# Two products opened together behind constant matmuls, and lo parts and last sums in another order

## The chip, the cores and the metric

The kernel runs on one core of a Trainium2 chip. The metric is the device time of one execution in microseconds (us), the median of several runs; less is better.

## The reference

Two layers of a streaming encoder work on 640 tokens (512 of a new stream, 8 × 16 of running ones) of width D = 1024. Each layer has a half feed-forward, a mixer and another half feed-forward. All is float32. Cut to what this change touches:

```python
def _rmsnorm(x, g):
    xf = x.astype(jnp.float32)
    y = xf * lax.rsqrt(jnp.mean(xf * xf, axis=-1, keepdims=True) + EPS)
    return y.astype(x.dtype) * g
def _swiglu(h, w_gu, w_down):
    gu = h @ w_gu
    g, u = jnp.split(gu, 2, axis=-1)
    return (jax.nn.silu(g) * u) @ w_down
...
    for l in range(DEPTH):            # DEPTH = 2, D_FF = 2816
        xp = xp + 0.5 * _swiglu(_rmsnorm(xp, norm_ffn1[l]), w_ffn1_gu[l], w_ffn1_down[l])
...
        xp = xp + mp                  # mixer: short convolution and banded attention
        xp = xp + 0.5 * _swiglu(_rmsnorm(xp, norm_ffn2[l]), w_ffn2_gu[l], w_ffn2_down[l])
```

## The kernel before, in words

**Layout and accuracy.** x lies transposed: eight blocks of 128 rows of D by 640 tokens. Each float32 operand of a matmul is split in a hi part, which ACT (ScalarE) casts, and a lo part, the rest, which DVE (VectorE) subtracts. A product of one 128 × 128 block is three products on PE (TensorE): hi·hi, lo·hi and hi·lo, each as two matmuls of 320 tokens. Names: `whi`, `wlo` are a slab's parts, `xhi`, `xlo` a block's. A trailing a or b in a name stands for the feed-forward ahead of or behind the mixer.

**Slabs.** Weights come from `wst` as slabs of 128 × 1024 that SP's queue loads into three `raw` buffers. Line 368 casts a slab's hi part on ACT at once. Its lo part is put in a list, which `flush` (line 374) hands to DVE when the program calls it. A slab in the set `fine` has its lo part cut in two halves there. Some slabs are sums or differences of others; DVE makes them (line 297), or a DMA that accumulates does, issued by POOL (`lent`, lines 276 and 277).

**Products by seven.** Past the opening, gate and up products of the feed-forward and the down products are made in a scheme with seven block products in place of eight. The kinds are X11, X21, XT5, XN6, XT7, X22 and XT4; X sums and differences of operands are made for it (`mixed`, `even`, `odd`, `rest`, `fourth`), and partial results in PSUM go to `c` tiles and into others.

**Down products.** `down_rows` adds a chunk's product to four rows of D. It runs X11, X21, XN6, XT5, XT7, X22, XT4 through the accumulators `da`, `db` and `dc`. A result goes to x in one of two ways: `take` (line 1196) is two DVE operations that add it straight from PSUM; `send` (line 1191) has ACT scale it into a tile and POOL issue two DMAs that add it to x. Two takes of `da` (columns t2, then t1), one of `dc`, and the sends of c1, c5, u2 belong to each group. The first half of `da` must be out before XT4 may write it: the matmul `daa<-t4hia` waits there. There are ten groups in each feed-forward, named by first chunk and first row (0_0, 0_4, 4_0, … 16_4).

**The opening** (line 752) is the first feed-forward's first eight products, plain ones, made while x arrives: product 0 over the eight x blocks, then 1, and so on, 48 matmuls each, through two accumulators, `po`. So product 2 waits until ACT has copied product 0 out (`out(0)`, line 786), product 3 for product 1's copy (line 794). A product takes the raw x; the norm's factor comes in later, on the results. Its sums of squares (ACT line 731, DVE line 297) are totalled over partitions by 20 small matmuls (`npsa`, line 552) within product 2, turned by DVE and spread by two matmuls (`nbca`, line 571) within product 3.

**Order.** PE's order is the program's. ACT's and DVE's are as written too for most of the program; for a part of it a scheduler sets them. SP's queue holds the loads in order, and POOL's holds the accumulating DMAs.

Of the kernel before, what the change touches and what calls it, by code (L numbers as in the profile page):

```python
# [16 lines left out]
P = 128  # L17
# [177 lines left out]
def trunk(ctx: ExitStack, tc: tile.TileContext, xin, wst, small, pbias, samplebias, kcache, vcache, gfin,  # L195
# [27 lines left out]
    def att(name):  # L223
        return banks["att"].tile([P, 512], F32, tag="att", name=name)
# [33 lines left out]
    raws, ready = [], []  # L258
    rows = [what == "rows" for l in range(L) for k in "ab" for what, _ in ffn_order(f"{k}{l}") if what in ("gu", "rows")]
    fine = {i + o for i, r, before in zip([i for i, z in enumerate(slabs) if z[0] == "gu" and z[2] == 0], rows,  # L260
                                          [False] + rows) if r for o in ((1, 3) if before else (3,))}
    sums, pool, spool = {}, [None], [None]
    lent, lean, at = {}, set(), 0
    for name, (_, units) in zip([f"{k}{l}" for l in range(L) for k in "amb"], stages()):
# [107 lines left out]
    def flush(n=None):  # L372
        for lo, src, hi in pending[:n]:
            DVE.tensor_tensor(out=lo, in0=src, in1=hi.bitcast(F32), op=ALU.subtract)  # L374
        del pending[:n]
# [20 lines left out]
    def ahead():  # L396

        source(len(ready))
# [92 lines left out]
    for k in range(KT):  # L491
        SP.dma_start(x[k], xin[:, k, :])

        if k == 0:
            raws.append(wp.tile([P, CH], F32, tag="raw", name="raw0", bufs=3))
        if k % 2 == 0:
            c = slice(k * P, (k + 2) * P)
            SP.dma_start(raws[0][:, c], wst[0][:, c])

    def norm(name, goff, ssum, keep):  # L500

# [82 lines left out]
    class Expand(Stats):  # L584
# [98 lines left out]
        def mixed(self, kp):  # L683

            n = f"{self.name}_{kp}"
            hi, lo = self.ops[kp]
            (e1, e2), (o1, o2) = ([x[2 * kp + i][:, c] for c in (slice(0, HT), slice(HT, T))] for i in range(2))
            ge, go = (sm[:, self.goff + 2 * kp + i :][:, 0:1] for i in range(2))
            no = less1[:, 2 * kp + 1 : 2 * kp + 2]
            E = self.fp.tile([P, 3, HT], F32, name=f"xe{n}", tag="even", bufs=1)  # L690

            def minus(out, a, g, b):
                DVE.scalar_tensor_tensor(out=out, in0=a, scalar=g, in1=b, op0=ALU.mult, op1=ALU.subtract)

            ACT.activation(E[:, 2], e2, AF.Copy, scale=ge)
            minus(E[:, 1], e1, ge, E[:, 2])
            self.flush()
            ACT.copy(hi[:, XT5], E[:, 1])
            self.late.append((lo[:, XT5], E[:, 1], hi[:, XT5]))
            yield  # L700
            self.flush()
            O = self.fp.tile([P, 5, HT], F32, name=f"xo{n}", tag="odd", bufs=1)
            minus(O[:, XN6], o2, no, E[:, 1])
            minus(O[:, XT4], o1, no, O[:, XN6])
            minus(O[:, XT7], o2, go, E[:, 2])
            ACT.copy(hi[:, 0:3], O[:, 0:3])
            self.late.append((lo[:, 0:3], O[:, 0:3], hi[:, 0:3]))
            yield
# [46 lines left out]
    def opening(fp, name, goff, n, pairs, tails):  # L755

        ACT.copy(early, epst)
        ex = Expand(fp, name, goff)  # L760
        h = []
        whi, wlo = (wp.tile([P, CH], F32R, tag=f"w{t}", name=f"w{t}0", bufs=3) for t in ("hi", "lo"))
        ready.append((whi, wlo))
        for k in range(KT):
            h.append(ex.plain(k))
            c = slice(k * P, (k + 2) * P)
            if k % 2 == 0:
                ACT.copy(whi[:, c], raws[0][:, c])
                DVE.tensor_tensor(out=wlo[:, c], in0=raws[0][:, c], in1=whi[:, c].bitcast(F32),
                                  op=ALU.subtract)  # L770
        flush()

        mixed = [z for kp in range(NP) for z in [ex.mixed(kp)] * 2]
        made = {2: (0, 1, 2), 3: (3,), 4: (4,), 5: (5, 6), 6: (7,)}
        us, gs, ps = [], [], []

        def out(i):

            j, up = divmod(i, 2)
            if not up:  # L780
                gs.append(tmp(f"g{name}_{j}"))
                if j:
                    scaled(gs[j], ps[i], ex.rho)
                    ACT.activation(gs[j], gs[j], AF.Silu)
                else:
                    ACT.copy(halves(gs[j]), two(ps[i]))
                return
            u = tmp(f"u{name}_{j}") if j > 1 else fp.tile([P, T], F32, tag="cap", name=f"u{name}_{j}", bufs=6)
            us.append(u)
            if j:  # L790
                scaled(u, ps[i], ex.rho)
                DVE.tensor_tensor(out=u, in0=u, in1=gs[j], op=ALU.mult)
            else:
                ACT.copy(halves(u), two(ps[i]))

        def begun():
            ex.total(att(f"nps{name}"))
            ex.root()
            ex.diagonal()

        at = {2: {4: begun}, 3: {1: lambda: ex.spread([att(f"nbc{name}_{a}")[:, :HT] for a in range(2)])}}
        for i in range(2 * n):
            ps.append(acc(f"po{name}_{i}"))
            product(ps[i], h, at.get(i, {}))
            if i > 1:
                out(i - 1)
            if i == 0:
                for k in range(KT):
                    ex.square(k)
                    ex.add()  # L810
                    if k == 1:
                        out(0)
                    if k == 4:
                        flush()
            if i == 1:
                continue
            if i == 3:
                g, u = gs[0], us[0]
                DVE.tensor_tensor(out=g, in0=g, in1=ex.rho, op=ALU.mult)
                ACT.activation(g, g, AF.Silu)  # L820
                DVE.tensor_tensor(out=u, in0=u, in1=ex.rho, op=ALU.mult)
            flush()
            for m in made.get(i, ()):
                next(mixed[m])
            if i == 3:
                DVE.tensor_tensor(out=u, in0=u, in1=g, op=ALU.mult)
            if i == 4:
                pairs[0].even(us[0])
            if i == 5:
                pairs[0].odd(us[1])  # L830
            if i == max(made):
                ex.flush()
                ahead()
                pairs[0].mixed()
                pairs[0].fourth()
            if i == 2 * n - 1:
                pairs[1].even(us[2])
        ahead()
        out(2 * n - 1)
        tails += [lambda: pairs[1].odd(us[3]), pairs[1].mixed, pairs[1].fourth]  # L840
        ex.rest = None
        return ex
# [46 lines left out]
    def gate_up(fp, n, ex, first, tails, put, j, pair, later, at, halve):  # L889
# [9 lines left out]
        def spot(name):  # L899
            step(later, f"g{at}{name}")  # L900
# [4 lines left out]
        both = cap("c1_")  # L905
        c1, u2, c5 = both[:, 0], both[:, 1], cap("c5_")[:, 0]
        rho = ex.rho
        early_down = False
        if first:

            new = not ex.known
# [34 lines left out]
                tails.clear()  # L946
            s2 = quiet()
            prep(len(ready))
            if new:
                flush()  # L950

            def third():
                mul(pc, s2, 1, X22, every, False, True)
# [2 lines left out]
            if new:  # L956
                third()
                ex.total(acc(f"nps{n}")[:, 0])
                ex.root()
                ex.diagonal()  # L960
                prep(len(ready))
            mul(pa, s2, 0, XT7, every, False, True)
            add(g[:, t2], pa, c5)
# [5 lines left out]
            if not new:  # L969
                third()  # L970
                prep(len(ready))
                flush()
                held.extend(tails)
                tails.clear()
            s3 = slab(True)[0]
        else:
# [13 lines left out]
            flush()  # L990
            mul(pa, s1, 0, XN6, every, False, True)
            ACT.copy(u2, pa)
            early_down = len(held) > 2
            for t in held[: 1 if early_down else None]:
                t()
            del held[: 1 if early_down else None]
# [6 lines left out]
            add(g[:, t2], pa, c5)  # L1003
            DVE.tensor_tensor(out=g[:, t2], in0=g[:, t2], in1=rho[:, t2], op=ALU.mult)
            flush()
            if early_down:
                held.pop(0)()
            ahead()
            mul(pc, s2, 1, X22, every, False, True)
            add(u[:, t2], pc, u2)  # L1010
# [5 lines left out]
        if early_down:  # L1016
            behind.append(silu)
        else:
            silu()
        spot("e7")  # L1020
        flush()

# [21 lines left out]
    class Pair:  # L1044
# [64 lines left out]
        def fourth(self):  # L1109

            hi, lo = (self.fp.tile([P, HT], F32R, tag=f"t4{i}{self.i}", name=f"t4{i}{self.name}", bufs=1)
                      for i in ("hi", "lo"))
            ACT.copy(hi, self.A[:, 1])
            self.low(lo, hi, self.A[:, 1])
            self.keep((XT4,), hi, lo)

        def low(self, lo, hi, z):
            DVE.tensor_tensor(out=lo, in0=z, in1=hi.bitcast(F32), op=ALU.subtract)
# [31 lines left out]
                next(p.work)  # L1150
                p.done += 1

    def down_rows(fp, n, ms, pairs, tails, later):


        A, B = (acc(f"d{i}{n}") for i in "ab")
# [36 lines left out]
        def take(ps, r, cols, scale=0.5):  # L1193
            for u in range(2):
                xs = x[ms[2 * u + r]][:, cols]
                DVE.scalar_tensor_tensor(out=xs, in0=ps[u], scalar=scale, in1=xs, op0=ALU.mult, op1=ALU.add)
# [36 lines left out]
        s3 = slab(True)[0]  # L1233
        ahead()
        mul(a, s3, 0, XT4, False)
        take(a, 1, t1, -0.5)
        flush()

    def ffn(name, fp, ex, goff, after, end=False):
# [54 lines left out]
        for what, a in ffn_order(name):  # L1294
# [20 lines left out]
                continue  # L1315
            if what == "rows":
                ms, js = a
                down_rows(fp, f"{name}_{js[0]}_{ms[0]}", ms, [pairs[j] for j in js[::2]], tails, later)
                continue
            js = a if what == "ends" else a[0][1]  # L1320
            if js[0] == last or len(a) * len(js) >= KT:
# [1148 lines left out]
```

## Time and profile before

| | before |
|---|---|
| median of 3 runs | 2471.61 us (2471.43 to 2471.65) |
| profiled execution | 2472.6 us |
| its span | 2470.8 us |
| instructions | 44076 |
| PE busy | 2458.0 us |
| DVE busy | 2195.4 us |
| ACT busy | 1399.7 us |
| POOL busy | 326.8 us |
| moved by DMA | 290.26 MB |

The profile shows one execution; its span runs from the first instruction to the last, and 1.8 us of the execution's time lie outside it. Times in a row are us from the start of the span. A row of a timeline gives start, duration, engine, line, operation, tiles, and in brackets the idle time ahead of it and what ended it; "x2" means two instructions put together. A matmul's duration is its whole passage and overlaps the next one's; the pace is read from starts. A row of the table by stretches gives for each engine the busy time and the number of instructions, then the granted clock of PE, the DMA share and GB/s. In a row of waits stand the engine and tile that waited, what it waited for, the total, the number and the longest.

### The profile page before, as it was taken

The page shows a single profiled execution, that of the slowest core. Times are in us where ns is not written, and L with a number is a line of the kernel's source. Part 1 is how long each engine was busy: PE and PEld are TensorE (multiplying, and loading weights), DVE is VectorE, ACT ScalarE, POOL GpSimd, SP SyncE. Part 2 cuts the span into 40 slices and gives each one's busy share as a digit, 9 for nine tenths or more (in the row PEclk, how much of TensorE's full clock was granted, in tenths as well). Part 3 has the DMA queues.
Part 4 walks back from the last instruction along what each step waited for, and adds up shares of the span by engine and source line. Part 5 has one row for each costly group of instructions (what it writes and reads, how often), then busy time and mean ns, then how long its engine had stood idle before and what let it go on. Part 6 is the DMA issues. An engine that isn't in the chain of part 4 may idle for free.

```text
span 2470.8 us, 44076 instructions
## 1 busy us (share of the span) xinstructions
PE 2458.0 (99%) x17216; PEld 2407.4 (97%) x17216; DVE 2195.4 (89%) x3726; ACT 1399.7 (57%) x2242; POOL 326.8 (13%) x491
## 2 busy tenths in 40 slices
PE   9999999999999999999999999999999999999999
PEld 8999999889999999999999999998899999999998
DVE  7999998888998899998799999998889989999997
ACT  6555556675565555555665555567656555555555
POOL 0110112211110001111001010121110000111111
PEclk9999999999999999999999999999999999999999
DMA  4443445335344334444334343452454433444444
GB/s 156 127 117 103 118 118 128 104 120 175 108 131 125 90 102 107 112 118 119 110 92 112 107 116 107 118 129 101 134 166 120 121 118 94 107 113 107 112 118 118
DMA packets 114273, 290.26 MB, mean 117 GB/s; under 512 B 13104, under 2 KB 52528, under 8 KB 114064
## 3 DMA queue, kind: packets, MB, share of 16 engines
q1 hardware_dynamic: 69408, 220.10, 27.9%
q0 software_dynamic: 44224, 67.09, 14.3%
q8 instruction: 135, 2.21, 0.4%
q14 instruction: 74, 0.61, 0.1%
q10 hardware_dynamic: 432, 0.25, 0.0%
HBM read 241.57 MB, written 7.94 MB: 101 GB/s over the span
## 4 chain that ended last, share of the span: by engine, by line
PE 96%; DVE 1%; ACT 1%; issue 1%; DMA 1%; ACTq 0%; SPq 0%; DVEq 0%; POOLq 0%
PE pab L468 12%; PE paa L468 11%; PE pcb L468 6%; PE pca L468 6%; PE daa L1169 5%; PE dab L1169 5%; PE po L444 5%; PE qa L468 4%; PE pbb L468 3%; PE pba L468 3%; PE dca L1169 3%; PE dcb L1169 2%; PE ma_cv L468 2%; PE ma_qk L468 2%; PE pv L1862 2%; PE poa L444 2%
## 5 line engine op out<-in xcount | busy, mean ns | idle before, releaser
L374 DVE TENSOR_TENSOR wlo<-raw,whi 128x1024 fp32r<-128x1024 f32 (+2 forms) x604 | 581.1, 970 | 156.5 <-ACT whi L368 153.1
L368 ACT CAST whi<-raw 128x512 fp32r<-128x512 f32 (+1 forms) x566 | 502.7, 893 | 374.8 <-PE pbb L468 47.2
L368 ACT CAST whi<-s 128x1024 fp32r<-128x1024 f32 (+1 forms) x166 | 155.6, 937 | 287.5 <-issue 109.0
L468 PE MATMUL pab<-xhib,whi 128*128 128x320 f32 x704 | 217.6, 309 | 0.0
L468 PE MATMUL pab<-xhib,wlo 128*128 128x320 f32 x704 | 217.2, 308 | 0.0
L468 PE MATMUL pab<-xlob,whi 128*128 128x320 f32 x704 | 217.2, 308 | 0.0
L468 PE MATMUL paa<-xhia,wlo 128*128 128x320 f32 x640 | 197.7, 309 | 0.2 <-DVE wlo L374 0.2
L468 PE MATMUL paa<-xhia,whi 128*128 128x320 f32 x640 | 197.9, 309 | 0.0
L468 PE MATMUL paa<-xloa,whi 128*128 128x320 f32 x640 | 197.7, 309 | 0.0
L374 DVE TENSOR_TENSOR wlo<-s,whi 128x1024 fp32r<-128x1024 f32 (+1 forms) x169 | 179.8, 1064 | 4.0 <-ACT whi L368 4.0
L1191 POOL DMA_DIRECT2D x<-c_a x80 | 70.0, 1021 | 575.6 <-ACT ahia L1070 203.8
L1191 POOL DMA_DIRECT2D x<-c_b x72 | 63.3, 1017 | 581.5 <-ACT ahib L1070 204.0
L468 PEld LDWEIGHTS pab<-xhib,whi 128*128 128x128 f32 x704 | 132.1, 188 | 0.9 <-issue 0.9
L468 PEld LDWEIGHTS pab<-xlob,whi 128*128 128x128 f32 x704 | 132.2, 188 | 0.0
L468 PEld LDWEIGHTS pab<-xhib,wlo 128*128 128x128 f32 x704 | 132.2, 188 | 0.0
L468 PEld LDWEIGHTS paa<-xhia,whi 128*128 128x128 f32 x640 | 120.1, 188 | 0.7 <-issue 0.4
L468 PEld LDWEIGHTS paa<-xhia,wlo 128*128 128x128 f32 x640 | 120.1, 188 | 0.6 <-DVE wlo L374 0.5
L468 PEld LDWEIGHTS paa<-xloa,whi 128*128 128x128 f32 x640 | 120.1, 188 | 0.3 <-DVE xloa L712 0.3
L297 DVE TENSOR_TENSOR raw<-s,raw 128x512 f32<-128x512 f32 x166 | 113.9, 686 | 0.0
L468 PE MATMUL pcb<-xhib,wlo 128*128 128x320 f32 x352 | 108.8, 309 | 0.0
L468 PE MATMUL pcb<-xhib,whi 128*128 128x320 f32 x352 | 108.6, 309 | 0.0
L468 PE MATMUL pcb<-xlob,whi 128*128 128x320 f32 x352 | 108.6, 309 | 0.0
(891 smaller groups left out, 8250.1 us busy)
## 6 DMA issues: line engine op xcount, KB each, us to landing
raw<-in_wst SPq DMA_DIRECT2D x375, 512.0 KB, 3.6
x<-c_a POOLq DMA_DIRECT2D x80, 160.0 KB, 4.4
x<-c_b POOLq DMA_DIRECT2D x72, 160.0 KB, 3.5
one<-in_wst POOLq DMA_DIRECT2D x40, 256.0 KB, 3.5
lent<-in_wst POOLq DMA_DIRECT2D x36, 256.0 KB, 3.9
kc<-in_kcache SPq DMA_DIRECT2D x32, 256.0 KB, 4.8
vc<-in_vcache SPq DMA_DIRECT2D x16, 512.0 KB, 4.4
x<-u_a POOLq DMA_DIRECT2D x40, 160.0 KB, 4.2
```

Of the source, the lines that this page charges most:

```text
L297: DVE.tensor_tensor(out=out, in0=a, in1=b, op=op)
L368: ACT.copy(hi[:, d], src[:, c])
L374: DVE.tensor_tensor(out=lo, in0=src, in1=hi.bitcast(F32), op=ALU.subtract)
L444: PE.matmul(ps[:, a, :HT], w, x[a] if isinstance(x, tuple) else x[:, a * HT : (a + 1) * HT], start=first and j == 0 and not seeded, stop=l ...
L468: PE.matmul(ps, a, b, start=start and kp == 0 and j == 0, stop=stop and kp == NP - 1 and j == 2, skip_group_check=True)
L1169: PE.matmul(ps[u], w, y, start=start and i == 0 and j == 0, stop=i == 1 and j == 2, skip_group_check=True)
L1191: POOL.dma_start(x[ms[2 * u + r]][:, cols], z[:, u], accum_op=ALU.add)
L1862: PE.matmul(pv[t], xx[:, t * P : (t + 1) * P], w[:, kk * AW : (kk + 1) * AW], start=c == 0 and kk == 0 and j == 0, stop=c == KT // 2 - 1 a ...
```

## The change

Five things change.

1. **Opening.** The second slab is loaded in four slices as the first is, and the slices of both go between the blocks of x, one behind each block. ACT and DVE split them in turn. Products 0 and 1 run together: for each pair of x blocks, 12 matmuls of product 0, then 12 of product 1. Ahead of them PE gets nine float32 matmuls of constants (`idle`; a row of ones that DVE sets, times the ones that POOL sets), whose result nobody reads. The squares follow, with the copies of the products 0 and 1 behind the fourth and fifth sum; the totals stand at step 6 of product 2, where they stood at step 4. The step in which the first two x operands of the mixed kind are made (`made`) comes one product later.
2. **`mixed`**: the lo parts of slabs are handed out ahead of the first `minus` operation (before: behind it), and then behind the last one (before: ahead of the last three).
3. **`fine`**: of a unit that follows a group of four rows, the slab that is cut in two is the one at offset 4, the next unit's first (128 × 1024), and no longer the one at offset 3 (the last, 128 × 512).
4. **`gate_up`, `fourth`**: behind the norm's sums the lo part of a slab comes after the turn of the sums (`diagonal`); the lo part of the t4 operand is made at another place.
5. **`down_rows`**: where the chunk is among the plain ones (groups 0_0 and 0_4 of the first feed-forward alone), the last result of `da` is sent by ACT and POOL, and no longer taken by DVE.

```diff
+WAKE = 9
...
-                                          [False] + rows) if r for o in ((1, 3) if before else (3,))}
+                                          [False] + rows) if r for o in ((1, 4) if before else (4,))}
...
         if k == 0:
-            raws.append(wp.tile([P, CH], F32, tag="raw", name="raw0", bufs=3))
-        if k % 2 == 0:
-            c = slice(k * P, (k + 2) * P)
-            SP.dma_start(raws[0][:, c], wst[0][:, c])
+            raws += [wp.tile([P, CH], F32, tag="raw", name=f"raw{i}", bufs=3) for i in range(2)]
+        c = slice(k // 2 * 2 * P, (k // 2 + 1) * 2 * P)
+        SP.dma_start(raws[k % 2][:, c], wst[k % 2][:, c])
...
             ACT.activation(E[:, 2], e2, AF.Copy, scale=ge)
+            self.flush()
             minus(E[:, 1], e1, ge, E[:, 2])
-            self.flush()
...
-            self.flush()
...
             minus(O[:, XT7], o2, go, E[:, 2])
+            self.flush()
...
+        idle, row = att("idle"), tmp("row")[:, :P]
+        DVE.memset(row, 1.0)
+        for i in range(WAKE):
+            PE.matmul(idle[:, :P], ones.to_broadcast([P, P]), row, start=i == 0, stop=i == WAKE - 1)
+        first = [acc(f"po{name}_{i}") for i in range(2)]
         for k in range(KT):
             h.append(ex.plain(k))
...
+            raw, (whi, wlo) = raws[k % 2], ready[k % 2]
+            ACT.copy(whi[:, c], raw[:, c])
+            DVE.tensor_tensor(out=wlo[:, c], in0=raw[:, c], in1=whi[:, c].bitcast(F32), op=ALU.subtract)
+            if k % 2:
+                for p, w in zip(first, ready):
+                    for kk in (k - 1, k):
+                        multiply(p, [z[:, kk * P : (kk + 1) * P] for z in w], h[kk], kk == 0, kk == KT - 1)
+        used[0] = 2
...
-        made = {2: (0, 1, 2), 3: (3,), 4: (4,), 5: (5, 6), 6: (7,)}
+        made = {2: (0,), 3: (1, 2, 3), 4: (4,), 5: (5, 6), 6: (7,)}
...
-        at = {2: {4: begun}, 3: {1: lambda: ex.spread([att(f"nbc{name}_{a}")[:, :HT] for a in range(2)])}}
-        for i in range(2 * n):
+        at = {2: {6: begun}, 3: {1: lambda: ex.spread([att(f"nbc{name}_{a}")[:, :HT] for a in range(2)])}}
+        prep(2)
+        flush()
+        for k in range(KT):
+            ex.square(k)
+            ex.add()
+            if k in (4, 5):
+                out(k - 4)
+        for i in range(2, 2 * n):
...
                 ex.diagonal()
+                flush()
                 prep(len(ready))
...
-            self.low(lo, hi, self.A[:, 1])
             self.keep((XT4,), hi, lo)
+            return lambda: self.low(lo, hi, self.A[:, 1])
...
-        take(a, 1, t1, -0.5)
+        if sent:
+            send(stage("t4_", A, -0.5), 1, t1)
+        else:
+            take(a, 1, t1, -0.5)
```

PE's order at the end of the first pair's blocks in product 0, before (`poa_0` and `poa_1` are products 0 and 1; `xhia_0`, `xhia_1` hold the first and second pair of x):

```order
L444 MATMUL poa_0_175<-xhia_0_131,whi_129 128x320 x2
L444 MATMUL poa_0_175<-xloa_0_132,whi_129 128x320 x2
L444 MATMUL poa_0_175<-xhia_0_131,wlo_130 128x320 x2
L444 MATMUL poa_0_175<-xhia_1_143,whi_129 128x320
L444 MATMUL poa_0_175<-x2hia_0_133,whi_129 128x320
L444 MATMUL poa_0_175<-xloa_1_144,whi_129 128x320
```

And now, at the same place:

```order
L445 MATMUL poa_0_150<-xhia_0_152,whi_134 128x320 x2
L445 MATMUL poa_0_150<-xloa_0_153,whi_134 128x320 x2
L445 MATMUL poa_0_150<-xhia_0_152,wlo_135 128x320 x2
L445 MATMUL poa_1_151<-xhia_0_152,whi_136 128x320
L445 MATMUL poa_1_151<-x2hia_0_154,whi_136 128x320
L445 MATMUL poa_1_151<-xloa_0_153,whi_136 128x320
```

Product 1's 12 matmuls with the first pair now stand here, ahead of product 0's with the second pair.

ACT's order behind the last block of x, before (`ssuma` and `sqa` are the norm's squares; `ga_0` is the copy of product 0):

```order
L668 ACTIVATE xhia_3_165<-x_99,sm 128x640
L368 CAST whi_178<-raw_176 128x512 x2
L368 CAST whi_186<-raw_184 128x1024
L728 ACTIVATE ssuma_127<-x_92 128x640
L731 ACTIVATE sqa_1_238<-x_93 128x640
L786 COPY ga_0_241<-poa_0_175 128x640
L731 ACTIVATE sqa_2_243<-x_94 128x640
L731 ACTIVATE sqa_3_246<-x_95 128x640
```

And now:

```order
L668 ACTIVATE xhia_3_264<-x_99,sm 128x640
L774 CAST whi_136<-raw_102 128x256
L369 CAST whi_302<-raw_300 128x1024
L728 ACTIVATE ssuma_132<-x_92 128x640
L731 ACTIVATE sqa_1_307<-x_93 128x640
L731 ACTIVATE sqa_2_310<-x_94 128x640
L731 ACTIVATE sqa_3_313<-x_95 128x640
L731 ACTIVATE sqa_4_316<-x_96 128x640
L795 COPY ga_0_319<-poa_0_150 128x640
L731 ACTIVATE sqa_5_321<-x_97 128x640
L803 COPY ua_0_324<-poa_1_151 128x640
```

The second slab's cast has gone from here (its slices stand between the x blocks), and the copy of product 0 stands behind three more squares.

DVE's order at the end of group 0_4 of the first feed-forward, before (the rows x<-daa and x<-dca are takes):

```order
L1118 TENSOR_TENSOR aloa_6_1428<-dea_6_1429,ahia_6_1427 128x640
L374 TENSOR_TENSOR wlo_1424<-raw_1421,whi_1423 128x1024
L1196 SCALAR_TENSOR_TENSOR x_97<-daa_0_4_1347,x_97 128x320
L1196 SCALAR_TENSOR_TENSOR x_99<-daa_0_4_1347,x_99 128x320
L1196 SCALAR_TENSOR_TENSOR x_96<-dca_0_4_0_1349,x_96 128x320
L1196 SCALAR_TENSOR_TENSOR x_98<-dca_0_4_1_1350,x_98 128x320
L297 TENSOR_TENSOR raw_1421<-s_18_1453,raw_1421 128x512
L374 TENSOR_TENSOR wlo_1473<-s_18_1453,whi_1472 128x1024
L1196 SCALAR_TENSOR_TENSOR x_97<-daa_0_4_1347,x_97 128x320
L1196 SCALAR_TENSOR_TENSOR x_99<-daa_0_4_1347,x_99 128x320
```

And now:

```order
L1124 TENSOR_TENSOR aloa_6_1448<-dea_6_1449,ahia_6_1447 128x640
L375 TENSOR_TENSOR wlo_1444<-raw_1441,whi_1443 128x512
L1202 SCALAR_TENSOR_TENSOR x_97<-daa_0_4_1368,x_97 128x320
L1202 SCALAR_TENSOR_TENSOR x_99<-daa_0_4_1368,x_99 128x320
L1202 SCALAR_TENSOR_TENSOR x_96<-dca_0_4_0_1370,x_96 128x320
L1202 SCALAR_TENSOR_TENSOR x_98<-dca_0_4_1_1371,x_98 128x320
L375 TENSOR_TENSOR wlo_1444<-raw_1441,whi_1443 128x512
L375 TENSOR_TENSOR wlo_1494<-s_18_1474,whi_1493 128x1024
L298 TENSOR_TENSOR raw_1441<-s_18_1474,raw_1441 128x512
```

The whole lo part of 128 × 1024 ahead of the takes is now two halves, one ahead and one behind them, and the last two takes of `daa` are gone.

More of the change, by code (lines that the diff above doesn't have):

```diff
@@ L761, in opening @@
         h = []
-        whi, wlo = (wp.tile([P, CH], F32R, tag=f"w{t}", name=f"w{t}0", bufs=3) for t in ("hi", "lo"))
-        ready.append((whi, wlo))
+        for i in range(2):
+            ready.append(tuple(wp.tile([P, CH], F32R, tag=f"w{t}", name=f"w{t}{i}", bufs=3) for t in ("hi", "lo")))
+        idle, row = att("idle"), tmp("row")[:, :P]
[3 more added lines that the diff above has]
+        first = [acc(f"po{name}_{i}") for i in range(2)]
         for k in range(KT):
             h.append(ex.plain(k))
[L766 to L771, printed above, removed]
+            c = slice(k // 2 * 2 * P, (k // 2 + 1) * 2 * P)
+            raw, (whi, wlo) = raws[k % 2], ready[k % 2]
[6 more added lines that the diff above has]
+        used[0] = 2
         mixed = [z for kp in range(NP) for z in [ex.mixed(kp)] * 2]
-        made = {2: (0, 1, 2), 3: (3,), 4: (4,), 5: (5, 6), 6: (7,)}
-        us, gs, ps = [], [], []
+        made = {2: (0,), 3: (1, 2, 3), 4: (4,), 5: (5, 6), 6: (7,)}
+        us, gs, ps = [], [], first
         def out(i):
@@ L799, in begun @@
             ex.diagonal()
-        at = {2: {4: begun}, 3: {1: lambda: ex.spread([att(f"nbc{name}_{a}")[:, :HT] for a in range(2)])}}
-        for i in range(2 * n):
+        at = {2: {6: begun}, 3: {1: lambda: ex.spread([att(f"nbc{name}_{a}")[:, :HT] for a in range(2)])}}
[7 more added lines that the diff above has]
+        for i in range(2, 2 * n):
             ps.append(acc(f"po{name}_{i}"))
             product(ps[i], h, at.get(i, {}))
-            if i > 1:
+            if i > 2:
                 out(i - 1)
[L807 to L816, printed above, removed]
             if i == 3:
@@ L831, in opening @@
             if i == max(made):
+                ahead()
                 ex.flush()
-                ahead()
                 pairs[0].mixed()
-                pairs[0].fourth()
+                pairs[0].fourth()()
             if i == 2 * n - 1:
@@ L907, in gate_up @@
         rho = ex.rho
-        early_down = False
+        early_down = low4 = None
         if first:
@@ L948, in gate_up @@
             prep(len(ready))
-            if new:
-                flush()
             def third():
@@ L972, in gate_up @@
                 flush()
+                low4 = tails.pop()()
                 held.extend(tails)
@@ L992, in gate_up @@
             ACT.copy(u2, pa)
-            early_down = len(held) > 2
+            early_down = len(held) > 1
             for t in held[: 1 if early_down else None]:
@@ L1005, in gate_up @@
             flush()
-            if early_down:
-                held.pop(0)()
             ahead()
@@ L1019, in gate_up @@
             silu()
+        if low4:
+            low4()
         spot("e7")
@@ L1151, in step, with down_rows @@
                 p.done += 1
-    def down_rows(fp, n, ms, pairs, tails, later):
+    def down_rows(fp, n, ms, pairs, tails, later, sent):
         A, B = (acc(f"d{i}{n}") for i in "ab")
@@ L1317, in ffn @@
                 ms, js = a
-                down_rows(fp, f"{name}_{js[0]}_{ms[0]}", ms, [pairs[j] for j in js[::2]], tails, later)
+                down_rows(fp, f"{name}_{js[0]}_{ms[0]}", ms, [pairs[j] for j in js[::2]], tails, later,
+                          js[0] < plain)
                 continue
```

## The prediction

> **What bounds the kernel now.** I read the page first, then the waits of the matmul engine, then the opening on each engine, and last the feed-forward stages in which the matmul engine waits. The page's busy rows, and the longest waits that the trace names for PE (in all, times, longest, us):
>
> ```profile
> span 2470.8 us, 44076 instructions
> PE 2458.0 (99%) x17216; PEld 2407.4 (97%) x17216; DVE 2195.4 (89%) x3726; ACT 1399.7 (57%) x2242; POOL 326.8 (13%) x491
> ...
> PE poa L444 <- ACT whi L768: 5.5, 1, 5.5
> PE daa L1169 <- DVE x L1196: 0.5, 2, 0.3
> PE paa L468 <- DVE wlo L374: 0.2, 1, 0.2
> PE dab L1169 <- DVE x L1196: 0.2, 1, 0.2
> ```
>
> PE is the bound from end to end: 2458.0 of 2470.8 us busy, 12.8 idle, of which 5.5 lie ahead of the first product. The change removes no product of data, so all it can win is idle time, and time in which PE runs slowly. Both are largest in the opening. PE there (start, duration, instruction, wait in brackets):
>
> ```profile
> 5.52 0.64 PE L444 MATMUL poa<-xhia,whi 128*128 128x320 f32 x1 [5.52 <-ACT whi L768]
> ...
> 9.69 0.42 PE L444 MATMUL poa<-x2loa,whi 128*128 128x320 f32 x1
> 9.95 0.31 PE L444 MATMUL poa<-xhia,wlo 128*128 128x320 f32 x1
> 10.10 0.31 PE L444 MATMUL poa<-x2hia,wlo 128*128 128x320 f32 x1
> ...
> 13.28 0.42 PE L444 MATMUL poa<-xhia,whi 128*128 128x320 f32 x1
> ...
> 14.93 0.56 PE L444 MATMUL poa<-xloa,whi 128*128 128x320 f32 x2 [0.16 <-DVE xloa L663]
> ...
> 15.63 0.31 PE L444 MATMUL poa<-xhia,whi 128*128 128x320 f32 x1
> ...
> 22.67 0.31 PE L444 MATMUL poa<-xhia,whi 128*128 128x320 f32 x1
> ```
>
> Until 9.95 the matmuls start 0.27 us apart (9.69, 9.95; 16 of them in the 4.43 us from 5.52), then 0.147 (9.95, 10.10; and 48 matmuls in 22.67 − 15.63 = 7.04). So the clock opens about 4.3 us after the first matmul, and product 0 also waits for x at 13.28 and 14.93. Product 1 starts at 15.63, product 2 at 22.67. Two products are 96 × 0.147 = 14.1 us, so from 5.52 they could end at 19.6: **3.05 us is all there is to win here**.
>
> **The opening.** The slices of raw0 first (KB each, median us from issue to landing), then ACT's rows that feed PE:
>
> ```profile
> raw<-in_wst SPq DMA_DIRECT2D x4, 128.0 KB, 5.0
> ...
> 5.08 0.39 ACT L768 CAST whi<-raw 128x256 fp32r<-128x256 f32 x1
> 5.58 0.83 ACT L668 ACTIVATE xhia<-x,sm 128x640 fp32r<-128x640 f32 x1
> ...
> 13.13 0.83 ACT L668 ACTIVATE xhia<-x,sm 128x640 fp32r<-128x640 f32 x1
> ...
> 17.02 0.73 ACT L731 ACTIVATE sqa<-x 128x640 f32<-128x640 f32 x1
> 17.65 0.67 ACT L786 COPY ga<-poa 128x640 f32<-128x640 f32 x1
> ...
> 22.36 1.99 ACT L368 CAST whi<-raw 128x1024 fp32r<-128x1024 f32 x2
> ```
>
> The first product still needs the first x block and the first slice of raw0, which stay at the head of SP's queue: 5.52 is unchanged. Later blocks of x land behind four slices of raw1, 4 × 128 KB. The stretch from 9.8 to 16 us moves 402 GB/s (its row is below), so 512 KB are 1.3 us, and the last block, whose hi part started at 13.13, is 1.1 to 1.3 later, about 14.3. This costs little, because each pair of blocks now carries 24 matmuls, 3.5 us, where it carried 12. ACT's work for a pair (0.5 + 0.5 + 0.4 + 0.83 + 0.4 = 2.6 us by these rows) fits within.
>
> The nine constant matmuls. Their inputs are set at about 1 us. No 128-column fp32 matmul is in the opening of before; the end of the kernel has two, as four records:
>
> ```profile
> 2457.94 0.49 PE L571 MATMUL nbcf<-fsum,ones 64*128 64x128 f32 x4
> ```
>
> 0.49 us for two, so at most 0.25 each, and 0.45 at the half clock (× 0.267 / 0.147): nine take 2.2 us if the clock were open and 4.0 if not. I take 4.0, the pace of before's first matmuls: from 1.05 to about 5.0. At either end they hold no one up, since data come at 5.52. Whether they open the clock is the question. In before it took 4.3 us of matmuls; counted from 1.05 that is 5.35, ahead of 5.52, but with a gap of half a us in it. I take it open by 5.52.
>
> [...]
>
> With an open clock the first six matmuls end at 6.4. DVE's rows for the second block of x and for a slice's lo part:
>
> ```profile
> 5.68 0.42 DVE L769 TENSOR_TENSOR wlo<-raw,whi 128x256 fp32r<-128x256 f32 x1
> 6.44 1.39 DVE L663 SCALAR_TENSOR_TENSOR xloa<-x,sm,xhia 128x640 fp32r<-128x640 f32 x2 [0.34 <-ACT xhia L668]
> ```
>
> Lo of the second block is ready at about 7.3 (6.44 + 0.85), and PE, which has two hi matmuls until 6.7, waits 0.6. After that it finds each pair ready: products end at 5.52 + 14.1 + 0.6 = 20.2. Product 2 needs the accumulator that the copy of product 0 frees, and that copy stands on ACT behind the last x, a slab's cast (1.0) and five squares (0.64 each): 14.3 + 0.8 + 0.4 + 1.0 + 3.2 = 19.7, and product 0 itself ends 1 us ahead of product 1; copy until about 20.4. So product 2 starts at 20.2 to 20.7, **2.0 to 2.5 earlier; I take 2.2**. Bounds: 2.9 with no wait, 1.0 with the clock as before (3.05 less the 16 matmuls × 0.12 = 1.95 that it costs, since slow matmuls hide the 0.6).
>
> The norm sums stand one pair later (26.28 in before; now about 25.6 to 26.2), and the spread, a step into product 3, comes at 28.7: no wait, 1.5 us spare. In `mixed`, a slab's lo part goes ahead of the first `minus` and the next one behind the last, and two of the blocks are made one product later; PE has 7 us per product there, so I price it at nothing; if that cover is gone it shows as a PE wait of at most one 1.22 us lo part, once.
>
> **The feed-forward waits.** The matmuls that started late, then what DVE did ahead of each:
>
> ```profile
> 102.74 0.41 PE L1169 MATMUL daa<-t4hia,whi 128*128 128x320 f32 x1 [0.26 <-DVE x L1196]
> 108.53 0.41 PE L468 MATMUL paa<-xhia,wlo 128*128 128x320 f32 x1 [0.24 <-DVE wlo L374]
> 128.06 0.41 PE L1169 MATMUL daa<-t4hia,whi 128*128 128x320 f32 x1 [0.19 <-DVE x L1196]
> 1159.92 0.42 PE L1169 MATMUL dab<-t4hib,whi 128*128 128x320 f32 x1 [0.20 <-DVE x L1196]
> ...
> 101.80 0.88 DVE L1196 SCALAR_TENSOR_TENSOR x<-daa,x 128x320 f32<-128x320 f32 x2
> 107.26 1.22 DVE L374 TENSOR_TENSOR wlo<-s,whi 128x1024 fp32r<-128x1024 f32 x1
> 125.98 1.23 DVE L374 TENSOR_TENSOR wlo<-raw,whi 128x1024 fp32r<-128x1024 f32 x1 [0.45 <-ACT whi L368]
> 127.12 0.88 DVE L1196 SCALAR_TENSOR_TENSOR x<-daa,x 128x320 f32<-128x320 f32 x2
> 1157.84 1.23 DVE L374 TENSOR_TENSOR wlo<-raw,whi 128x1024 fp32r<-128x1024 f32 x1 [0.45 <-ACT whi L368]
> 1158.98 0.88 DVE L1196 SCALAR_TENSOR_TENSOR x<-dab,x 128x320 f32<-128x320 f32 x2
> ```
>
> Each such start costs its whole gap (its start less that of the matmul before and the pace: 0.36 to 0.42) and 0.10 more, since the next one follows 0.25 behind instead of 0.147: 0.46 to 0.52, **1.95 for the four**. At 128.06 and 1159.92 the sums from PSUM stand behind a lo part of 1.23; cut in two, only the first half (0.69, with 0.09 of overlap) stands ahead and the sums are 0.54 earlier, more than the 0.36 missing. At 102.74 the sums stand ahead of that lo part already, so the cut does not help; there DVE itself is late:
>
> ```profile
> 9.80:16.00 6.20, 5.93 (x37) 5.25 (x36) 5.82 (x11) 5.23 (x10) 0.90 (x1) 1.00 1.04 402
> 85.00:95.00 10.00, 10.00 (x71) 10.00 (x70) 9.84 (x18) 4.99 (x9) 1.99 (x3) 1.00 0.58 169
> 95.00:105.00 10.00, 9.74 (x67) 9.48 (x66) 9.93 (x18) 5.03 (x9) 3.83 (x5) 1.00 0.63 172
> ...
> 62.81 1.16 DVE L712 TENSOR_TENSOR xloa<-xoa,xhia 128x960 fp32r<-128x960 f32 x1 [1.06 <-ACT xhia L706]
> ```
>
> DVE (third busy figure) has 9.84 and 9.93 of 10 us: whatever it gains ahead of 85 it keeps, relative to PE. There it waits for ACT between the blocks that `mixed` makes (1.06 at 62.81); the lo part of a slab now stands in that gap. I estimate from that row some 0.8 us, beyond PE's own 2.2. At 108.53 it also has two sums less (0.88), given to ACT and POOL. That store's two accumulating DMAs stand on POOL ahead of the next loaded sum, which then lands some 1.7 us later, with about 11 us to spare before ACT casts it. So all four go: −1.95.
>
> The flush moved behind the diagonal, and the later t4 lo parts, act on small gaps only:
>
> ```profile
> 399.51 0.41 PE L1169 MATMUL daa<-t4hia,whi 128*128 128x320 f32 x1
> 1252.82 0.81 PE L571 MATMUL nbca<-ssuma,ones 64*128 64x320 f32 x4
> ```
>
> 1252.82 (0.2: the turned sums stood behind a 1.22 lo part, now ahead) goes; 399.51 stays, as both halves still stand ahead of its sums; other starts of the last product of a group, late by less than the trace calls a wait, may give 0 to 0.5. I take 0.45 for all of these.
>
> **Sum.** 2.2 + 1.95 + 0.45 = 4.6. The profiled execution took 2472.6, 1.8 outside its span of 2470.8 and 1.0 above the median of 2471.61; it comes to 2468.0, and the median to **2467.0**. A measurement of this kernel can tell about 0.2% from no change, 4.94 us, that is below 2466.67 or above 2476.55.
>
> **Rivals.** A: the constants do not open the clock (the gap ahead of 5.52 speaks for it, the 4.0 us of work against). The opening gives 1.0; the rest stays: 2468.2. Chance 0.2. B: DVE does not keep what the opening wins, since PE runs 2.2 us ahead of it and DVE has 9.9 of 10 us from 85 to 105; the two waits at 102.74 and 108.53 stay or grow to 1 us each: 2.2 + 0.93 + 0.45 − 1.0 = 2.6, 2469.0. Chance 0.15. C: no wait in the opening and every small gap gone: 2.9 + 1.95 + 1.0 = 5.85, 2465.8. Chance 0.17. D, slower: the second half of the cut lo part stands behind the sums, and the product that reads it comes too early. There are ten groups of four rows of D in each of four feed-forwards. From the start of the sums the half is done after 0.88 + 0.88 + 0.6 = 2.4 us; PE's last product starts after 0.9, takes 12 × 0.147 = 1.8, and the first half of the slab serves 1.8 more: it is needed at 4.5. So it decides once something (ACT's cast, a buffer) holds that half 2.1 us longer; at 0.25 us in each of 40 groups it costs 10: 2477.0. DVE's 89% speaks against it. Chance 0.04. The forecast has 0.44.
>
> **Range and chances.** 2465.6 to 2469.6 holds the forecast (2466.2 to 2467.8), C, A and B. Faster: C with 0.17 and 0.18 of the forecast, its part below 2466.67: 0.35; slower: D, of which I give 0.03 to more than 0.2%; the same: 0.62.
>
> **What would show it.** PE's first matmul of data at 5.5 with 0.147 behind it; the first one of product 2 at 20.2 to 20.7; no wait at the four places, each about 2 to 4 us earlier in time; DVE's halves of 0.69 with sums between. Starts of 0.27 apart after 5.5 would mean A; PE waits for lo parts between 85 and 130, B; a wait for a second half in many groups, D. I would be wrong in the whole if product 2 starts later than 22, or if PE waits at places that it does not wait at now.

## The result, and the profile after

The changed kernel takes 2467.78 us, median of 22 runs (2467.01 to 2469.37); the kernel before takes 2471.63 beside it (22 runs, 2471.2 to 2472.04). The ratio is 0.9985, 95% interval [0.9978, 0.9991]: 3.85 us less where 4.6 were forecast, and within 0.2% of no change, as forecast. The profiled execution took 2468.21, 4.39 below that of before. From its page:

```profile
span 2466.4 us, 44136 instructions
PE 2458.3 (100%) x17234; PEld 2409.1 (98%) x17234; DVE 2196.8 (89%) x3725; ACT 1396.9 (57%) x2246; POOL 329.7 (13%) x495
```

PE's busy time holds 4.2 us of constants now, and its idle time fell from 12.8 to 8.1. The longest waits of PE (in all, times, longest):

```profile
PE idle L768 <- POOL epst L484: 1.1, 1, 1.1
PE poa L445 <- ACT ga L795: 0.7, 1, 0.7
PE poa L445 <- ACT whi L774: 0.3, 1, 0.3
PE poa L445 <- DVE xloa L663: 0.3, 1, 0.3
```

None of the old waits for x or `wlo` in the feed-forwards is in the list, and a new one is, in the opening: product 2 waits for `ga`, ACT's copy of product 0. PE in the opening:

```profile
1.15 4.17 PE L768 MATMUL idle<-row,ones 128*128 128x128 f32 x18 [1.15 <-POOL epst L484]
5.63 0.41 PE L445 MATMUL poa<-xhia,whi 128*128 128x320 f32 x1 [0.31 <-ACT whi L774]
...
6.32 0.36 PE L445 MATMUL poa<-xhia,wlo 128*128 128x320 f32 x1
...
7.38 0.56 PE L445 MATMUL poa<-xloa,whi 128*128 128x320 f32 x2 [0.26 <-DVE xloa L663]
...
20.08 0.46 PE L445 MATMUL poa<-xhia,wlo 128*128 128x320 f32 x2
21.19 0.41 PE L445 MATMUL poa<-xhia,whi 128*128 128x320 f32 x1 [0.65 <-ACT ga L795]
```

The nine constants are 18 records of 0.23 us, 4.17 in all where 4.0 were forecast at the slow pace; the first product runs at the full one (four matmuls between 5.63 and 6.32 cover 0.69, with 0.10 lost behind the first, so 0.147 each). Product 2 could follow at 20.37, and PE starts it at 21.19, when ACT has done this:

```profile
14.84 0.83 ACT L668 ACTIVATE xhia<-x,sm 128x640 fp32r<-128x640 f32 x1
15.57 0.39 ACT L774 CAST whi<-raw 128x256 fp32r<-128x256 f32 x1
16.36 1.05 ACT L369 CAST whi<-raw 128x1024 fp32r<-128x1024 f32 x1 [0.40 <-DMA raw<-in_wst]
17.32 0.73 ACT L728 ACTIVATE ssuma<-x 128x640 f32<-128x640 f32 x1
17.96 2.61 ACT L731 ACTIVATE sqa<-x 128x640 f32<-128x640 f32 x4
20.47 0.67 ACT L795 COPY ga<-poa 128x640 f32<-128x640 f32 x1
```

Where the time came from can be read place by place, since both traces hold the same matmuls of data in nearly the same order. The lead is the time of a matmul in before less its time in the changed kernel:

| place (its time in before) | lead behind it | gained there |
|---|---|---|
| second matmul of product 2 (22.82) | 1.37 | 1.37 |
| 66 to 83 | 1.58 | 0.21 |
| 102.74, sums of 0_0 | 1.70 | 0.12 |
| 108.53, lo part | 2.21 | 0.51 |
| 128.06, sums of 0_4 | 2.67 | 0.46 |
| up to 325.50 | 2.77 | 0.10 |
| 399.51, sums of 16_0 | 3.12 | 0.35 |
| 1159.92, sums of 12_4 | 3.79 | 0.67, of it 0.46 at the place |
| 1252.82, spread | 4.07 | 0.28 |
| up to 1858.54, second mixer | 4.29 | 0.22 |
| 1858.69, the same mixer | 3.98 | −0.31 |
| last matmuls (2464.5) | 4.06 | 0.08 |

The last 0.33 of the 4.39 lie behind the last matmul, in the landing of the output's last transfers. At 1858.69 PE is late in the changed kernel and was not in before; two more profiles of the changed kernel (e4 and e12 below) do not lose this. And the sum belongs to this pair of executions: that of before was 1.0 above its median, that of the changed kernel 0.4 above its own.

A row of PE, and DVE's rows around it and around the sums of 0_4, answer to those shown of before:

```profile
101.04 0.42 PE L1175 MATMUL daa<-t4hia,whi 128*128 128x320 f32 x1
...
100.11 0.88 DVE L1202 SCALAR_TENSOR_TENSOR x<-daa,x 128x320 f32<-128x320 f32 x2
100.91 1.28 DVE L375 TENSOR_TENSOR wlo<-raw,whi 128x512 fp32r<-128x512 f32 x2
...
123.76 0.69 DVE L375 TENSOR_TENSOR wlo<-raw,whi 128x512 fp32r<-128x512 f32 x1 [0.44 <-ACT whi L369]
124.37 0.88 DVE L1202 SCALAR_TENSOR_TENSOR x<-daa,x 128x320 f32<-128x320 f32 x2
...
126.10 0.68 DVE L375 TENSOR_TENSOR wlo<-raw,whi 128x512 fp32r<-128x512 f32 x1
```

At 124 one half of the lo part stands ahead of the sums and one behind all four, as the order says, and no wait of PE is left. At 101.04 PE still loses 0.39 us (0.28 and 0.11 behind it): DVE's sums are 1.7 us earlier than in before, and so is PE.

### The profile page after: what moved, and what is told of

Same layout as the page of the kernel before. It is cut to its first block, busy times and chain, and to the rows that moved or that the text cites. A ratio compares the mean times of both kernels' runs of the same rounds, so it can differ in the third digit from the quotient of the medians.

```text
span 2466.4 us, 44136 instructions
## 1 busy us (share of the span) xinstructions
PE 2458.3 (100%) x17234; PEld 2409.1 (98%) x17234; DVE 2196.8 (89%) x3725; ACT 1396.9 (57%) x2246; POOL 329.7 (13%) x495
## 3 DMA queue, kind: packets, MB, share of 16 engines
q8 instruction: 135, 2.21, 0.4%
## 4 chain that ended last, share of the span: by engine, by line
PE 97%; DMA 1%; DVE 1%; ACT 0%; issue 0%; SPq 0%; DVEq 0%; ACTq 0%
PE pab L469 13%; PE paa L469 11%; PE pcb L469 6%; PE pca L469 6%; PE daa L1175 6%; PE dab L1175 5%; PE po L445 5%; PE qa L469 4%; PE pbb L469 3%; PE pba L469 3%; PE dca L1175 3%; PE dcb L1175 3%; PE ma_qk L469 2%; PE ma_cv L469 2%; PE pv L1872 2%; PE qc L469 2%
## 5 line engine op out<-in xcount | busy, mean ns | idle before, releaser
L369 ACT CAST whi<-raw 128x1024 fp32r<-128x1024 f32 (+1 forms) x564 | 500.1, 892 | 376.1 <-DVE raw L298 63.6
L375 DVE TENSOR_TENSOR wlo<-raw,whi 128x1024 fp32r<-128x1024 f32 (+1 forms) x602 | 580.0, 967 | 135.4 <-ACT whi L369 131.8
L469 PE MATMUL pcb<-xlob,whi 128*128 128x320 f32 x352 | 108.5, 308 | 0.0
L469 PE MATMUL pcb<-xhib,whi 128*128 128x320 f32 x352 | 108.5, 308 | 0.0
```

What stands on the lines that cost most here:

```text
L369: ACT.copy(hi[:, d], src[:, c])
L469: PE.matmul(ps, a, b, start=start and kp == 0 and j == 0, stop=stop and kp == NP - 1 and j == 2, skip_group_check=True)
```

## The experiments

Theory 1: product 2 starts when ACT has copied product 0, and that copy stands behind a slab's cast and five squares; the feed-forward waits went each for its own reason, the cut and the sent sums. The rivals: PE's own pace sets the opening, and DVE's lead, won in the opening, took the waits away. Each time below is the median of 11 runs, with the kernel before beside it (32 or 33 runs on that chip). The runs stand in three groups: e1 to e4 (before: 2472.12), e5, e6, e7 and e9 (2471.81), and e8 and e10 to e12 (2471.86). One kernel's runs scatter by 0.3 to 1.0 (standard deviation), so a difference of a few tenths between two medians says nothing.

**The changed kernel without the constants** (e1):

```diff
-WAKE = 9
...
-        idle, row = att("idle"), tmp("row")[:, :P]
-        DVE.memset(row, 1.0)
-        for i in range(WAKE):
-            PE.matmul(idle[:, :P], ones.to_broadcast([P, P]), row, start=i == 0, stop=i == WAKE - 1)
```

> The changed kernel without the nine constant matmuls. Theory 1 (ACT's queue: product 2 waits for the copy of product 0, which stands behind a slab's cast and five squares): the clock opens some 4.3 us after 5.6 as before, so some 16 matmuls cost 0.12 us each, 1.9 us, less the 0.4 that PE now waits for the second block's lo part and less the 0.9 that it waits for the copy; product 2 starts at 21.6 to 21.8 where it started at 21.19, and the time is 0.4 to 0.7 above the changed kernel's, about 2468.3. Rival (PE's own matmuls set the start of product 2): the whole 1.9 us comes back, about 2469.6.

2468.86, 1.05 above the changed kernel on that chip (2467.81, e4 below): more than the 0.4 to 0.7 of theory 1, less than the 1.9 of the rival. In its profile the clock opens near 8.9, which here and below means that the matmuls start 0.147 us apart from then on and 0.27 until then:

```profile
8.36 0.74 PE L444 MATMUL poa<-xhia,wlo 128*128 128x320 f32 x2
8.89 0.38 PE L444 MATMUL poa<-xhia,whi 128*128 128x320 f32 x1
9.11 0.31 PE L444 MATMUL poa<-x2hia,whi 128*128 128x320 f32 x1
```

Product 2 starts at 21.27 there, without a wait for the copy, and so hardly later than in the changed kernel. This execution (2468.31) is the second fastest of the kernel's eleven, so it does not show where the 1.05 of the medians lies.

**The copy of product 0 two squares earlier** (e2, and again as e11 with the same edit):

```diff
-            if k in (4, 5):
-                out(k - 4)
+            if k in (2, 5):
+                out(k // 5)
```

> The changed kernel with the copy of product 0 behind the third sum of squares instead of the fifth, so two squares of 0.64 us stand behind it on ACT. Theory 1: the copy is done before product 1 ends, product 2 starts at 20.2 to 20.4 where it started at 21.19, and the time falls by 0.8 to 0.9, to about 2466.9; the spread over the runs shrinks too, if it comes from late loads that move ACT's queue. Rival (DVE, with over 9.5 of 10 us busy from 70 to 105, sets the pace there): product 2 is earlier, but the gain is given back as a longer wait at 101, and the time stays at 2467.8.

> The early copy of product 0 once more, beside the changed kernel on one chip. Theory 1 in its mended form: product 2 starts at the later of the end of product 1 on PE and the copy; with the early copy it starts at 20.2 to 20.9, with where in that by the moment at which the clock opens, so the median is 0.3 to 0.6 below the changed kernel's. Rival: the two medians agree within 0.2 again, and what the opening wins is lost after it.

2467.89 and 2467.61. In e2's profile the copy is done before PE needs it:

```profile
17.46 1.35 ACT L731 ACTIVATE sqa<-x 128x640 f32<-128x640 f32 x2
19.00 0.69 ACT L795 COPY ga<-poa 128x640 f32<-128x640 f32 x1 [0.18 <-PE poa L445]
19.59 1.99 ACT L731 ACTIVATE sqa<-x 128x640 f32<-128x640 f32 x3
...
20.27 0.46 PE L445 MATMUL poa<-xhia,wlo 128*128 128x320 f32 x2
20.56 0.31 PE L445 MATMUL poa<-xhia,whi 128*128 128x320 f32 x1
```

**The changed kernel again**, unedited, on the chips of the others (e4 and e12):

> The changed kernel once more, on the chip of the other three: 2467.8, and a second profile of its opening. Theory 1: the start of product 2 is at 20.9 to 21.5 in it, moved by the landing of the last x block and of the third slab; if the clock's opening sets it, matmuls 0.27 us apart are seen after 5.6 in a run that is slower.

> The changed kernel on the chip of the other three: 2467.8, product 2 at 20.9 to 21.3.

2467.81 and 2467.57; product 2 at 21.11 and 20.79. So the wait is as theory 1 has it: it is gone with the early copy, and product 2 starts at 20.56 and 20.42, 0.55 and 0.37 ahead of its neighbours. But the medians do not follow: 2467.89 against 2467.81, 2467.61 against 2467.57. The gain of 0.8 to 0.9, and the mended 0.3 to 0.6, were not measured. Nor are they all excluded: drawing the eleven runs of each kernel again and again gives differences from −0.7 to 0.8 in the first pair and from −0.45 to 0.2 in the second. In the profiled executions, 2467.53 and 2467.44 against 2467.88 and 2467.57, the gain is 0.35 and 0.13, and the lead shows the rival at work there: of 0.65 and 0.47 that the early copy leads by within product 2, 0.41 and 0.12 are left at the last matmul. 0.14 of the loss is at about 370 in both, just behind a copy by ACT (`c_a<-pca`), the rest in small pieces. What the early copy is worth stays open.

**Early copy and no constants** (both edits, e3):

> Both: no constant matmuls, and the copy of product 0 behind the third sum of squares. Theory 1: product 2 starts where PE's slow matmuls let it, 21.6 to 21.8, so the time is that of the kernel without constants, about 2468.3; set against the kernel with the early copy alone, the constants are then worth 1.4 us, and in the changed kernel 0.5. Rival (the constants are worth the same in both): 1.9 us above the early copy alone, and as far above the changed kernel when they are left out there.

2468.74; in this profile the slow pace lasts to 10.8 and product 2 starts at 22.12. The constants are worth 1.05 in the changed kernel (2468.86 less 2467.81) and 0.85 with the early copy (2468.74 less 2467.89). So neither 0.5 and 1.4 nor 1.9 twice: they are worth about 1 us in either. Theory 1 is right about the wait and wrong about this price.

**Four constants** (e10):

```diff
-WAKE = 9
+WAKE = 4
```

> The changed kernel with four constant matmuls instead of nine: they end near 3.0 us, 2.6 us ahead of the first product. [...]

2468.75, 1.18 above the changed kernel on that chip, so the same as without any. PE:

```profile
1.15 2.04 PE L768 MATMUL idle<-row,ones 128*128 128x128 f32 x8 [1.15 <-POOL epst L484]
5.42 0.63 PE L445 MATMUL poa<-xhia,whi 128*128 128x320 f32 x1 [2.23 <-ACT whi L774]
...
8.79 0.46 PE L445 MATMUL poa<-xhia,whi 128*128 128x320 f32 x1
9.05 0.34 PE L445 MATMUL poa<-x2hia,whi 128*128 128x320 f32 x1
```

Work that ends 2.2 us ahead of the products bought nothing here: the clock opens 3.6 us after 5.42. The nine constants ended at most 0.4 us ahead of the first product in all profiles but e5's, where they ran through faster.

**The old cut** (offset 3, e5):

```diff
-                                          [False] + rows) if r for o in ((1, 4) if before else (4,))}
+                                          [False] + rows) if r for o in ((1, 3) if before else (3,))}
```

> The changed kernel with the old choice of the slab that is cut in two (offset 3, no longer 4). Theory: the whole lo part of 1.22 us stands again ahead of the sums at the end of groups 0_4, 16_0 and, in the second feed-forward, 12_4; the three waits of 0.36 to 0.50 us come back at about 125.8, 397 and 1157, and some small ones, 1.2 to 1.5 us in all, 2469.1. Rival: DVE is ahead by what the opening won, and the waits do not come back (at most 0.3 us, 2468.0).

2469.1, 2.7 below the kernel before beside it, where the changed kernel is 3.85 to 4.3 below: 1.1 to 1.6 more (the changed kernel did not run in this group; against 2467.81 it is 1.3). DVE and PE in its profile:

```profile
123.35 1.23 DVE L375 TENSOR_TENSOR wlo<-raw,whi 128x1024 fp32r<-128x1024 f32 x1 [0.45 <-ACT whi L369]
124.49 0.88 DVE L1202 SCALAR_TENSOR_TENSOR x<-daa,x 128x320 f32<-128x320 f32 x2
...
125.43 0.41 PE L1175 MATMUL daa<-t4hia,whi 128*128 128x320 f32 x1 [0.19 <-DVE x L1202]
...
1156.83 0.41 PE L1175 MATMUL dab<-t4hib,whi 128*128 128x320 f32 x1 [0.19 <-DVE x L1202]
```

Two of the three waits are back (0.46 and 0.45 by the lead, against e4), with 0.1 here and there; the one at 397 is not. The rival falls: DVE's lead does not hide a whole lo part.

**The last sums taken by DVE** (e6):

```diff
-        if sent:
-            send(stage("t4_", A, -0.5), 1, t1)
-        else:
-            take(a, 1, t1, -0.5)
+        take(a, 1, t1, -0.5)
```

> The changed kernel with the last sums of the groups 0_0 and 0_4 taken by DVE again, not sent by ACT and POOL. Theory: two sums of 0.44 us stand ahead of the lo part that the matmul at 106.4 needs, and the wait of 0.4 to 0.5 us there comes back, 2468.3; the wait at 101.04 is ahead of them and stays as it is. Rival: DVE's lead hides the sums, and the time stays at 2467.8.

2468.84, 1.0 above 2467.81 (0.9 to 1.3 by the kernel before). The wait is back, and it is 0.57 by the lead. Against e4's profile 0.24 more is lost at 478.85, in the first mixer. The rest alone (e9, below) loses 0.27 at the same place with the sums sent, so that is not the edit's.

```profile
106.85 0.42 PE L469 MATMUL paa<-xhia,wlo 128*128 128x320 f32 x1 [0.31 <-DVE wlo L375]
107.11 0.32 PE L469 MATMUL paa<-xhia,whi 128*128 128x320 f32 x1
```

**The opening alone** (e7: before, with the new opening and `mixed`) and **the rest alone** (e9: before, with all but these):

> The kernel before with the new opening and the new order in the mixed operands alone: old cut, sums taken, old flush behind the norm's sums. Theory (the parts add up): product 2 starts 1.4 to 2.1 us earlier than in the kernel before, the waits at 102.7, 108.5, 128, 399 and 1160 all stay but for 0.1 to 0.2 us, so it is 1.4 to 2.2 below the kernel before. Rival (DVE keeps what it wins ahead of 85): the waits at 102.7 and 108.5 go too, 2.4 to 3.2 below.

> The kernel before with all of the change but the opening and the order in the mixed operands: new cut, sent sums, moved flush and t4 lo parts. Theory (the parts add up): the waits at 108.5, 128, 399, 1160 and 1253 go, that at 102.7 stays, 2.2 to 2.6 below the kernel before. Rival (the opening's lead is needed): at 108.5 and 128 DVE is still late, and it is only 1.0 to 1.4 below.

2470.41 and 2469.93, 1.40 and 1.88 below the kernel before; together 3.28, against 3.85 to 4.3 for the whole (the runs of e7 scatter by 0.95). By the lead at the last matmul they make 1.87 and 2.53, together 4.40, against 4.06, 4.39 and 4.70 in the three profiles of the whole; 0.35 at 399.51 is counted in both parts. The late matmuls of the opening alone:

```profile
101.26 0.42 PE L1175 MATMUL daa<-t4hia,whi 128*128 128x320 f32 x1 [0.26 <-DVE x L1202]
107.05 0.41 PE L469 MATMUL paa<-xhia,wlo 128*128 128x320 f32 x1 [0.24 <-DVE wlo L375]
126.57 0.41 PE L1175 MATMUL daa<-t4hia,whi 128*128 128x320 f32 x1 [0.19 <-DVE x L1202]
```

These are the waits of before (0.26, 0.24, 0.19), only 1.5 us earlier. In the rest alone, none of the four is in the list of waits, and by the lead it gains 0.5 at 108.5, 0.46 at 128, 0.48 at 1160 and 0.26 at the spread without any help of the opening, and 0.13 at 102.7. As far as these runs can tell, the parts add up.

**A further sum sent** (e8: the early copy, and in group 0_0 the sum that holds 101.04):

```diff
-        with soon():
-            take(a, 1, t2, -0.5)
+        if sent and not second:
+            send(stage("t7_", A, -0.5), 1, t2)
+        else:
+            with soon():
+                take(a, 1, t2, -0.5)
```

> The early copy of product 0, and in group 0_0 the other sum of da (the one that the matmul at 101.04 waits for) is sent by ACT and POOL too, no longer taken by DVE. Theory: ACT is idle from 98.5 there, the result leaves PSUM by 99.6, and the wait of 0.28 and 0.11 us goes: 0.4 below the early copy alone. Rival: the two more accumulating DMAs hold POOL's queue, a loaded sum lands later, and a wait for it comes in the same stage: no gain.

2468.53, 0.92 above the early copy alone. The late start at 101 goes (0.40 won there by the lead over e11), and 1.38 is lost just behind it, at 106.24. ACT, POOL and PE of this kernel:

```profile
102.07 1.05 ACT L369 CAST whi<-s 128x1024 fp32r<-128x1024 f32 x1 [3.23 <-DVE s L298]
104.16 0.71 ACT L1189 ACTIVATE t_a<-daa 128x640 f32<-128x640 f32 x1 [1.05 <-DMA x<-c_a]
105.76 0.43 ACT L985 COPY c_a<-paa 128x320 f32<-128x320 f32 x1 [0.89 <-DMA x<-t_a]
...
102.89 2.44 POOL L1197 DMA_DIRECT2D x<-u_a  x1
106.10 0.85 POOL L1197 DMA_DIRECT2D x<-c_a  x1 [0.77 <-DMA x<-t_a]
...
106.24 0.41 PE L469 MATMUL paa<-xhia,whi 128*128 128x320 f32 x1 [1.11 <-ACT c_a L985]
```

The rival was right that it is given back, but not by a loaded sum: ACT waits for a tile. The staged results share six buffers with other copies such as `c_a`, each is held until its accumulating DMA has landed, and a DMA that adds to a row of x waits for the one before on that row (0.77 at 106.10). One more send, and ACT's next two copies wait 1.05 and 0.89 for such a landing, and PE 1.11 for the second copy. None of the versions tried beats the changed kernel measurably.

## Why the prediction was right or wrong

- **PE bounds, and only idle or slow time can be won: right.** The gain is in PE's waits and in its slow matmuls, but for the 0.33 behind the last matmul.
- **The sum came out near, in part by luck.** The profiles hold 4.39 where 4.6 were forecast, but the opening gave 0.83 less than its term and the four places 1.55 and not 1.95. The other places gave 1.14 where 0.45 stood, of it 0.35 at a place that no part of the change explains, and 0.33 came behind the last matmul, where nothing was forecast.
- **The opening: right in kind, too large in size** (2.2 forecast, 1.37 in the profile, 1.45 and 1.77 in e4's and e12's, 1.40 by the opening alone). Product 2 was to start at 20.2 to 20.7; it started at 21.19, 21.11 and 20.79. The term named the chain that ends last, ACT's copy, and mis-sized it: the copy began at 20.47, not 19.7. Of these 0.77, 0.54 are the start of the last block's hi part, at 14.84 and not 14.3, and 0.23 the way from there to the copy, 5.63 and not 5.4: the third slab's cast waited 0.40 for its load, which the sum did not have, and the other pieces came out 0.17 shorter. The wait for `ga` is also a wait at a place where before had none, which the prediction named as a sign of being wrong in the whole; but it is the end of the chain that the term was added up from. The late start goes with slower loads: the stretch from 5.5 to 9.8 us moved 314 GB/s here and 380 in before. In e8, with the same slices, it moved 382, and the hi part started at 14.11. This kernel, then e8:

```profile
5.50:9.80 4.30, 3.91 (x24) 3.60 (x25) 3.70 (x8) 3.49 (x8) 1.62 (x4) 1.00 0.97 314
...
5.50:9.80 4.30, 4.22 (x24) 3.96 (x25) 3.07 (x8) 3.33 (x7) 1.34 (x3) 1.00 1.01 382
```

  The runs here do not show that the slices of 128 KB were the cause, since with the same eight slices this stretch moved 302 (e7) to 382 GB/s (e8). What made it slower in some executions stays open.
  Of the prediction's bounds, the lower was added up as 1.0; 3.05 less 1.95 is 1.1.
- **The clock: right in this profile.** It was to be open by 5.52, and the first product runs at the full pace, 0.147 (from 5.63 on); in five other executions with nine constants it opened 0.4 to 1.3 us after the first product's start.
- **The sums at 128.06 and 1159.92: right** (0.46 at each), by the cut, as e5 shows. **108.53: right** (0.51), by the two sums sent, as e6 shows, and not by DVE's lead.
- **102.74: wrong.** 0.12 of 0.52 was won. The step that failed is the 0.8 us that DVE was to gain "beyond PE's own" and to keep from 85 on. The wait at 62.81 did go, and gave about that. But what DVE led by ahead of it was not PE's lead. DVE's rows on both sides of that wait, in before and then in the opening alone:

```profile
61.20 0.55 DVE L693 SCALAR_TENSOR_TENSOR xoa<-x,sm,xea 128x320 f32<-128x320 f32 x1
65.22 0.82 DVE L1118 TENSOR_TENSOR tloa<-pba,thia 128x640 fp32r<-128x640 f32 x1
...
60.48 0.55 DVE L693 SCALAR_TENSOR_TENSOR xoa<-x,sm,xea 128x320 f32<-128x320 f32 x1
63.74 0.82 DVE L1124 TENSOR_TENSOR tloa<-pba,thia 128x640 fp32r<-128x640 f32 x1
```

  DVE led by 0.72 ahead of the place and by 1.48 behind it, and it kept 1.47 up to the sums (100.33 for 101.80). PE led by 1.27 there and by 1.40 from 79 on. So next to nothing was left beyond PE's own, and the wait stayed at 0.26. In the changed kernel DVE's sums are 1.69 earlier and PE, ahead of the wait, 1.56, hence the 0.12. That was in rival B's direction, without its further loss.
- **1252.82 went** (0.28), as forecast. **399.51 went too** (0.35), where I had it stay. It went also with the opening alone, with the rest alone and with the old cut, and with four constants it is there again:

```profile
396.76 0.41 PE L1175 MATMUL daa<-t4hia,whi 128*128 128x320 f32 x1 [0.17 <-DVE x L1202]
```

  So it belongs to no one part of the change, and it may come and go from execution to execution; no two profiles of one kernel show that. That a wait of one profile is a wait of every run was taken for granted in the sum.
- **Rival A** did not come. Its price was about right: 1.2 forecast, 1.05 and 0.85 by the kernels without constants; its time was not, 2468.2 against their 2468.86 and 2468.74. **D** did not come: second halves stand behind the sums (126.10) and no one waits for them.
- The median lies inside the range, and the forecast's own range (2466.2 to 2467.8) just holds it.

## What to carry to other kernels

When a transfer or a clock at the start is hidden, look at which queue then ends last: here ACT's, with a copy behind five squares, which took back 0.82 of the 2.30 us that product 2 could have come earlier in the profile. Then measure what that wait is worth: taking it away moved no median measurably. Cut the operation that stands ahead of the one that empties a PSUM accumulator, and do not count on its engine being early: DVE's lead was worth nothing at the waits, half a lo part 0.5 us at each. And align two traces matmul by matmul before explaining a difference: the lead shows each gain at its place, also those that no part of the change made.

## What the runs showed of the hardware

By the pace of the matmuls, the clock opens at another moment in each execution. With nine constants from 1.15 on it opened inside the constants in one (e5: they take 3.70 instead of 4.17, and the pace changes at 4.1), by 5.7 in the changed kernel's first profile, e6 and e7, and after a few slow matmuls of data, at 6.0 to 6.8, in e4, e12, e11, e8 and e2. Without them, or with four, it opened at 8.9, 9.1, 9.1, 9.95 and 10.8 (e1, e10, e9, before, e3). That is 3 to 5.7 us after the work begins that reaches to the products. What sets the moment was not shown. In e10, with 2.2 us between the last constant and the first product, it came at 9.1, as without constants; with nine, and gaps of up to 0.4 us there (0.8 in e5, where it came at 4.1), by 6.8 at the latest.

The profile's granted clock does not show this: in e3 the stretch in which all matmuls start 0.27 apart reads 1.00 (the third figure from the end of the row).

```profile
5.60:10.70 5.10, 5.10 (x19) 5.10 (x20) 4.68 (x10) 4.46 (x10) 1.11 (x2) 1.00 1.02 357
```
